# Hybrid decoder layer: the gated linear attention heads' matmuls on the whole 128 x 128 array, two chunks together

## The chip, the core and the metric

The kernel runs on one core of one Trainium2 chip. The engines of the core are named as the profile names them: PE (TensorE, with PEld for its weight loads), DVE (VectorE), ACT (ScalarE), POOL (GpSimd) and SP, which issues DMAs. The metric is the device time of one execution in microseconds (us); lower is better. TensorE's clock is granted at one of two levels, 2.4 GHz (1.00 in the profile) and 1.2 GHz (0.50).

## What is computed

One decoder layer: an input projection, two groups of heads side by side (a gated linear recurrence, HGRN2, and a sparse attention), an output projection, a mixture of experts, and a gate. The change touches the recurrence alone. It has 4 heads of 128 keys and 128 values, and 512 tokens in 8 chunks of 64:

```python
G = jnp.cumsum(chunks(log_f, HG_DK), axis=3)
G_ref, G_last = G[:, :, :, C // 2 - 1:C // 2], G[:, :, :, C - 1:C]
causal = jnp.tril(jnp.ones((C, C), dtype=bool))
a = jnp.einsum('bhntk,bhnsk->bhnts', qc * jnp.exp(G - G_ref), kc * jnp.exp(G_ref - G))
o_intra = jnp.einsum('bhnts,bhnsv->bhntv', jnp.where(causal, a, 0.0), vc)
def step(S, xs):                     # over chunks; k_t = kc*exp(G_last-G), q_t = qc*exp(G)
    q_t, k_t, v_t, d_t = xs
    o_t = jnp.einsum('bhtk,bhkv->bhtv', q_t, S)
    S = d_t[..., None] * S + jnp.einsum('bhtk,bhtv->bhkv', k_t, v_t)
    return S, o_t
```

The output of a head is `o_intra` plus the `o_t` of the scan, then an RMS norm and a gate.

## The kernel before

The layer runs in stages. A first stage projects the 512 tokens onto the columns of the input weights. Each projection is done in three matmuls of reduced-precision parts (`mm3`, lines 181 to 183: high by high, low by high, high by low), 128 x 128 weights against 512 columns; they write tiles named `mm`. The weights come by DMA into `wraw`, ACT makes the high part (`whi`, line 186) and DVE the low part (`wlo`, line 187).

Into this stage the four heads of the recurrence are placed, in the order head 0, head 1, the projection of keys and values (`kv_cols`), head 2, head 3. A list scheduler lays out one static order per engine when the program is built; each engine works strictly through its own row and waits on semaphores where an operand isn't ready. It puts projection matmuls between those of the heads where it expects a wait.

One head (`hg_head`) does this in plain fp32. DVE and ACT make the decayed keys and queries `k1`, `q1`, `k2`, `q2` (lines 368 to 386). Then, for tokens on partitions, two chunks lie side by side in one 128-row tile, the even chunk in rows 0 to 63 and the odd one in rows 64 to 127 (`po = 64 * (n % 2)`):

- line 391: 8 score matmuls, 64 x 64 each, into PSUM tile `at_ps` (named `hx`); line 393: DVE copies the causal part with `copy_predicated` into `AT`, whose other entries were zeroed once;
- line 396: 4 transposes of `k2` into `kt_ps` (the same single PSUM buffer `hx`); line 398: ACT copies them to `kT`, two buffers;
- line 404: 7 matmuls of the state's increments, 64 rows of `kT` against 64 rows of `hv`, into two PSUM tiles `u_ps` in turn; lines 406 and 408: DVE updates the state `St[n]` from `St[n-1]`;
- lines 414 and 415: 7 matmuls `q2` x `St` and 8 matmuls `AT` x `hv`, each for one chunk, into 64 partitions of `o_ps`;
- line 417 (ACT), 419 (DVE), the POOL lines 175 to 178 and line 423 (DVE): norm and gate of the head.

In the records, an fp32 matmul leaves two matmul rows and two weight loads, a transpose one. A row writes a matmul as out<-moving,weights with the array's rows * columns that it uses: `64*64` is a quarter of the array.

Of the kernel before, what the change touches and what calls it, by code (L numbers as in the profile page):

```python
# [10 lines left out]
F32 = mybir.dt.float32  # L11
# [68 lines left out]
def _shape_constants():  # L80
    f = np.float32
    c = np.zeros((128, C_END), f)
    c[:, C_ID:C_ID + 128] = np.eye(128, dtype=f)
    c[:, C_SCAN:C_SCAN + T] = (np.arange(T) % CH != 0).astype(f)[None, :]
    p = np.arange(128)
    c[:, C_CAUS:C_CAUS + 128] = np.where(p[None, :] <= p[:, None], 0.0, NEG)
    n = np.arange(32)
    for tt in range(NT):
        ok = ((tt * 128 + p)[:, None] >= (16 * n + 31)[None, :]) & (n < NCMP)[None, :]
        c[:, C_CADD + 32 * tt:C_CADD + 32 * (tt + 1)] = np.where(ok, 0.0, NEG)  # L90
        c[:, C_C01 + 32 * tt:C_C01 + 32 * (tt + 1)] = ok
    c[:, C_IOTA:C_IOTA + 128] = p[None, :]
    c[:, C_ST:C_ST + 16] = np.array(STARTS[:16])[None, :]
    c[:, C_ST + 16] = 0.0
    c[:, C_ST + 17:C_ST + 32] = np.diff(np.array(STARTS[:16]))[None, :]
    tri = (p[:, None] % 64 <= np.arange(64)[None, :]).astype(np.uint32)
    tri = np.ascontiguousarray(np.broadcast_to(tri[:, None, :], (128, 4, 64)).reshape(128, 256))
    sl = 2.0 ** -np.arange(1.0, QH + 1)
    t = np.arange(T)
    al = np.zeros((2, QH * T + T + 32), f)  # L100
    al[0, :QH * T] = np.repeat(sl, T)
    al[1, :QH * T] = (-sl[:, None] * t[None, :]).reshape(-1)
    al[0, QH * T:QH * T + T] = t
# [51 lines left out]
def _body(ctx, tc, a, out, dbg=None):  # L155
    nc = tc.nc
    V, S, G, PE = nc.vector, nc.scalar, nc.gpsimd, nc.tensor
    act = S.activation
# [11 lines left out]
    hv, nq = hn[:, 0], hn[:, 1]  # L170
# [18 lines left out]
    def flat(ap):  # L189
        return ap.rearrange("p a b -> p (a b)")  # L190
# [10 lines left out]
    with ExitStack() as e2:  # L201
        e0 = ExitStack()
        wst = e2.enter_context(tc.tile_pool(name="wst", bufs=2, side="right", reuse_waits="tile"))
        proj = e0.enter_context(tc.tile_pool(name="proj", bufs=1, reuse_waits="tile"))
# [151 lines left out]
                act(sg[:, tt], gl, AF.Tanh, scale=0.5)  # L356
                V.scalar_tensor_tensor(sg[:, tt], sg[:, tt], 1.0, gl, op0=ALU.add, op1=ALU.mult)

        tri = proj.tile([128, 256], U32, name="tri")
        nc.sync.dma_start(out=tri, in_=a["tri"])  # L360
        ATs = [proj.tile([128, 4, CH], F32, name=f"AT{i}") for i in range(2)]
        for t_ in ATs:
            G.memset(t_, 0.0)
        qc = -0.5 * 128 ** -0.5

        def hg_head(h):
            Gt = lf[:, h].rearrange("p (n c) -> p n c", c=CH)
            V.tensor_tensor_scan(lf[:, h], cst[:, C_SCAN:C_SCAN + T], lf[:, h], 0.0, op0=ALU.mult, op1=ALU.add)
            d1 = hgp.tile([128, NCH, CH], F32, name="d1")
            V.tensor_tensor(d1, Gt, Gt[:, :, CH // 2 - 1:CH // 2].to_broadcast([128, NCH, CH]), op=ALU.subtract)  # L370
            d2 = hgp.tile([128, NCH, CH], F32, name="d2")
            V.tensor_tensor(d2, Gt[:, :, CH - 1:CH].to_broadcast([128, NCH, CH]), Gt, op=ALU.subtract)
            k1 = hgp.tile([128, T], F32, name="k1")
            act(k1, flat(d1), AF.Exp, scale=-1.0)
            q1 = flat(d1)
            act(q1, q1, AF.Exp)
            k2 = flat(d2)
            act(k2, k2, AF.Exp)
            act(Gt, Gt, AF.Exp)
            dk = hgp.tile([128, NCH], F32, name="dk")  # L380
            V.tensor_copy(dk, Gt[:, :, CH - 1])
            q2 = lf[:, h]
            V.scalar_tensor_tensor(q1, q1, qc, qs[:, h], op0=ALU.mult, op1=ALU.mult)
            V.scalar_tensor_tensor(k1, fg[:, h], 1.0, k1, op0=ALU.subtract, op1=ALU.mult)
            V.scalar_tensor_tensor(k2, fg[:, h], 1.0, k2, op0=ALU.subtract, op1=ALU.mult)
            V.scalar_tensor_tensor(q2, q2, qc, qs[:, h], op0=ALU.mult, op1=ALU.mult)
            at_ps = hps.tile([128, 512], F32, name="hx")
            for n in range(NCH):
                po = 64 * (n % 2)
                cs = slice(n * CH, (n + 1) * CH)  # L390
                PE.matmul(at_ps[po:po + 64, (n // 2) * CH:(n // 2 + 1) * CH], lhsT=k1[:, cs], rhs=q1[:, cs], start=True, stop=True)
            AT = ATs[h % 2]
            V.copy_predicated(flat(AT), tri, at_ps[:, :256])
            kt_ps = hps.tile([128, 512], F32, name="hx")
            for tt in range(NT):
                PE.transpose(kt_ps[:, tt * 128:(tt + 1) * 128], k2[:, tt * 128:(tt + 1) * 128], ident)
            kT = hgp.tile([128, NT, 128], F32, name="kT")
            act(flat(kT), kt_ps, AF.Copy)
            St = hgp.tile([128, NCH - 1, 128], F32, name="St")
            u_ps = [hps.tile([128, 512], F32, name=f"u_ps{k}") for k in range(2)]  # L400
            for n in range(NCH - 1):
                po = 64 * (n % 2)
                us = u_ps[n % 2][:, (n // 2) * 128:(n // 2 + 1) * 128]
                PE.matmul(us, lhsT=kT[po:po + 64, n // 2, :], rhs=hv[po:po + 64, n // 2, h * 128:(h + 1) * 128], start=True, stop=True)
                if n == 0:
                    V.tensor_copy(St[:, 0], us)
                else:
                    V.scalar_tensor_tensor(St[:, n], St[:, n - 1], dk[:, n:n + 1], us, op0=ALU.mult, op1=ALU.add)
            o_ps = hps.tile([128, NT, 128], F32, name="o_ps")
            for n in range(NCH):  # L410
                po = 64 * (n % 2)
                o = o_ps[po:po + 64, n // 2, :]
                if n:
                    PE.matmul(o, lhsT=q2[:, n * CH:(n + 1) * CH], rhs=St[:, n - 1], start=True, stop=False)
                PE.matmul(o, lhsT=AT[po:po + 64, n // 2, :], rhs=hv[po:po + 64, n // 2, h * 128:(h + 1) * 128], start=(n == 0), stop=True)
# [812 lines left out]
```

## Time and profile before

| What | us |
|---|---|
| median of 3 runs (1738.06 to 1745.13) | 1738.25 |
| the profiled execution, its own time | 1738.71 |
| its span, first to last instruction | 1737.0 |
| PE busy in the span | 1682.5 |
| stretch with the four heads | 101.74 to 181.44 |

The profile is one execution. Its rows give a start and a duration for each instruction (a row can merge several of one line); PE's rows overlap, since matmuls are pipelined, so the time that one costs is read from start to start. Idle time in front of an instruction stands in square brackets with what ended it; "issue" means that the profile shows nothing that was waited for.

### The profile page before, as it was taken

How to read it: one execution, taken by the hardware profiler on the slowest of the kernel's cores; microseconds unless marked ns; L12 is line 12 of the kernel's file. 1: busy time of each engine (PE TensorE's matmuls, PEld its weight loads, DVE VectorE, ACT ScalarE, POOL GpSimd, SP SyncE). 2: the span in 40 equal slices, each digit the busy share in tenths (PEclk: the TensorE clock that was granted, in tenths of full speed). 3: DMA queues.
4: the chain of work that ended last, by engine and by line, in shares of the span. 5: the costliest groups of instructions: out<-in, count | busy, mean ns of one | idle time of the engine just before them, and what ended most of it. 6: DMA issues, size and time to landing. Idle time of an engine off the chain costs nothing.

```text
span 1737.0 us, 24222 instructions
## 1 busy us (share of the span) xinstructions
PE 1682.5 (97%) x8959; PEld 1430.6 (82%) x8959; DVE 1253.3 (72%) x2442; ACT 742.4 (43%) x1276; POOL 475.8 (27%) x353
## 2 busy tenths in 40 slices
PE   7999999998999999999999999999999999999998
PEld 6866788877885667877899999999999999999987
DVE  5553555556999998594568877787787788888863
ACT  6432555444213985453343333333333333333342
POOL 0001300012000000100035556455554455455510
PEclk9998999889999999999999999999999999999999
DMA  7311022012212679977669888989898999999841
GB/s 254 102 49 27 28 84 63 13 51 96 73 49 62 185 233 267 317 255 253 211 232 331 319 318 324 341 307 324 326 317 315 332 322 325 348 333 336 315 133 49
DMA packets 147303, 374.30 MB, mean 215 GB/s; under 512 B 11670, under 2 KB 60438, under 8 KB 147182
## 3 DMA queue, kind: packets, MB, share of 16 engines
q1 hardware_dynamic: 108608, 232.90, 39.8%
q0 software_dynamic: 38576, 139.86, 22.7%
q8 instruction: 70, 1.15, 0.3%
q14 instruction: 49, 0.40, 0.1%
HBM read 339.42 MB, written 33.29 MB: 215 GB/s over the span
## 4 chain that ended last, share of the span: by engine, by line
PE 80%; DVE 8%; DMA 6%; ACT 3%; issue 2%; SPq 1%; POOL 0%; DVEq 0%; ACTq 0%; POOLq 0%
PE ac L183 9%; PE ac L182 9%; PE ac L181 9%; PE apsum L181 8%; PE apsum L183 8%; PE apsum L182 8%; PE mm L181 5%; PE mm L182 5%; PE mm L183 5%; PE ob L660 2%; DMA ga<-gd 2%; PE apsum L783 2%; DMA ur<-uT 2%; PE pt L657 1%; PE tp L183 1%
## 5 line engine op out<-in xcount | busy, mean ns | idle before, releaser
L183 PE MATMUL ac<-vh,pl 128*128 128x512 f32 x768 | 300.8, 392 | 2.8 <-DVE pl L187 2.8
L181 PE MATMUL ac<-vh,ph 128*128 128x512 f32 x768 | 298.1, 390 | 2.6 <-ACT ph L186 2.6
L182 PE MATMUL ac<-vl,ph 128*128 128x512 f32 x768 | 300.6, 392 | 0.0
L1032 POOL DMA_INDIRECT row<-u,eid x128 | 214.1, 1673 | 310.9 <-DVE hn L1036 243.2
L181 PE MATMUL apsum<-aTh,uh 128*128 128x384 f32 x864 | 290.8, 337 | 2.2 <-ACT ga L788 2.2
L183 PE MATMUL apsum<-aTh,ul 128*128 128x384 f32 x864 | 289.3, 335 | 1.5 <-DVE ul L187 1.4
L182 PE MATMUL apsum<-aTl,uh 128*128 128x384 f32 x864 | 288.7, 334 | 0.0
L1032 POOL DMA_INDIRECT row<-v,eid x128 | 203.7, 1592 | 186.1 <-DVE hn L1044 161.0
L186 ACT ACTIVATE uh<-ur 128x1024 fp32r<-128x1024 f32 x108 | 114.7, 1062 | 281.6 <-PE apsum L182 262.7
L187 DVE TENSOR_TENSOR ul<-ur,uh 128x1024 fp32r<-128x1024 f32 x108 | 132.1, 1224 | 87.6 <-ACT uh L186 87.3
L183 PEld LDWEIGHTS ac<-vh,pl 128*128 128x128 f32 x768 | 144.0, 188 | 34.5 <-DVE pl L187 4.2
L186 ACT ACTIVATE vh<-vr 128x1024 fp32r<-128x1024 f32 x128 | 135.4, 1058 | 86.5 <-PE ac L183 81.6
L181 PEld LDWEIGHTS ac<-vh,ph 128*128 128x128 f32 x768 | 144.1, 188 | 30.9 <-ACT ph L186 3.2
L1044 DVE SCALAR_TENSOR_TENSOR hn<-row,cw__6982,hn 128x1024 f32<-128x1024 f32 x128 | 158.3, 1280 | 14.9 <-DMA row<-v,eid 14.9
L182 PEld LDWEIGHTS ac<-vl,ph 128*128 128x128 f32 x768 | 144.0, 188 | 28.7 <-DVE vl L187 0.5
L181 PEld LDWEIGHTS apsum<-aTh,uh 128*128 128x128 f32 x864 | 162.2, 188 | 6.3 <-ACT ga L788 2.5
L182 PEld LDWEIGHTS apsum<-aTl,uh 128*128 128x128 f32 x864 | 162.3, 188 | 4.0
L183 PEld LDWEIGHTS apsum<-aTh,ul 128*128 128x128 f32 x864 | 162.2, 188 | 2.4 <-DVE ul L187 2.3
L187 DVE TENSOR_TENSOR vl<-vr,vh 128x1024 fp32r<-128x1024 f32 x128 | 156.1, 1219 | 9.9 <-ACT vh L186 9.8
L1036 DVE SCALAR_TENSOR_TENSOR hn<-row,hn 128x1024 f32<-128x1024 f32 x128 | 156.2, 1221 | 5.6 <-DMA row<-u,eid 4.2
L186 ACT ACTIVATE ph<-ga 128x384 fp32r<-128x384 f32 x118 | 62.0, 525 | 202.3 <-DVE ga L1096 147.7
L783 PE MATMUL apsum<-xf,ur 128*128 128x384 f32 x320 | 112.8, 497 | 7.7 <-DMA ur<-uT 7.7
(384 smaller groups left out, 2934.9 us busy)
## 6 DMA issues: line engine op xcount, KB each, us to landing
vr<-v SPq DMA_DIRECT2D x128, 512.0 KB, 5.5
ur<-uT SPq DMA_DIRECT2D x125, 512.0 KB, 6.6
wt<-wd SPq DMA_DIRECT2D x32, 768.0 KB, 7.4
wraw<-wi SPq DMA_DIRECT2D x24, 512.0 KB, 4.6
wd<-hn SPq DMA_DIRECT2D x5, 1664.0 KB, 8.9
wd<-stage SPq DMA_DIRECT2D x5, 1664.0 KB, 9.1
wr<-wq SPq DMA_DIRECT2D x16, 512.0 KB, 3.6
wor<-wo SPq DMA_DIRECT2D x8, 512.0 KB, 3.6
```

Of the source, the lines that this page charges most:

```text
L181: PE.matmul(o, lhsT=lh, rhs=rh, start=first, stop=False)
L182: PE.matmul(o, lhsT=lh, rhs=rl, start=False, stop=False)
L183: return PE.matmul(o, lhsT=ll, rhs=rh, start=False, stop=last)
L186: act(hi, src, AF.Copy)
L187: return V.tensor_tensor(lo, src, hi.bitcast(F32), op=ALU.subtract)
L657: PE.transpose(pt_ps[:, k * 128:(k + 1) * 128], P[:, k * 128:(k + 1) * 128], ident)
L660: PE.matmul(o_ps[:, h], lhsT=pt[:, k * 128:(k + 1) * 128], rhs=kv[:, k, 256 + i * 64:256 + (i + 1) * 64], start=(k == 0), stop=(k == tt))
L783: PE.matmul(o[:, :TD], lhsT=ur[:, c], rhs=xf[:, c], start=c == 0, stop=c == NC - 1)
L1032: G.indirect_dma_start(out=gt, out_offset=None, in_=table, in_offset=bass.IndirectOffsetOnAxis(ap=eid[:, slot:slot + 1], axis=0))
L1036: V.scalar_tensor_tensor(junk, gt, 1.0, xn0, op0=ALU.mult, op1=ALU.mult, accum_out=dots[:, s_:s_ + 1])
L1044: V.scalar_tensor_tensor(ak, gt, cw_[:, s_:s_ + 1], ak, op0=ALU.mult, op1=ALU.add)
```

## The change

The recurrence of a head is done for two chunks (128 tokens) at a time, so that every matmul has 128 rows and 128 columns of the array.

- Scores: 4 matmuls of 128 x 128 instead of 8 of 64 x 64. The mask `tri` becomes block-diagonal and twice as wide (512 columns), and `copy_predicated` takes 512 columns instead of 256.
- `kT` gets a dimension for the chunk's parity. The transposed keys of the even chunk stand in rows 0 to 63 of one half, those of the odd chunk in rows 64 to 127 of the other, and zeros elsewhere. ACT copies the one, DVE the other. `kT` is now one buffer for all heads, zeroed once by POOL. The 7 increments stay 7 matmuls.
- `q2` gets the same treatment along the token columns: it is written in two halves by DVE into a zeroed buffer (the one that was `xsq`), one for all heads, instead of in place over `lf`.
- Output: per 128 tokens one matmul `AT` x `hv` and two (one for the first tile) with the padded `q2` and the states of both chunks, accumulated in the same 128 partitions: 4 and 7 instead of 8 and 7.

```diff
-    tri = (p[:, None] % 64 <= np.arange(64)[None, :]).astype(np.uint32)
-    tri = np.ascontiguousarray(np.broadcast_to(tri[:, None, :], (128, 4, 64)).reshape(128, 256))
+    tri = ((p[:, None] // CH == p[None, :] // CH) & (p[:, None] <= p[None, :])).astype(np.uint32)
+    tri = np.ascontiguousarray(np.broadcast_to(tri[:, None, :], (128, NT, 128)).reshape(128, T))
...
-        ATs = [proj.tile([128, 4, CH], F32, name=f"AT{i}") for i in range(2)]
-        for t_ in ATs:
+        ATs = [proj.tile([128, NT, 128], F32, name=f"AT{i}") for i in range(2)]
+        kT = proj.tile([128, NT, 2, 128], F32, name="kT")
+        q2 = sm.tile([128, D], F32, name="xsq", bufs=1).rearrange("p (t c i) -> p t c i", t=NT, c=2)
+        for t_ in ATs + [kT, q2]:
             G.memset(t_, 0.0)
...
-            q2 = lf[:, h]
-            V.scalar_tensor_tensor(q2, q2, qc, qs[:, h], op0=ALU.mult, op1=ALU.mult)
+            quad = lambda x: x.rearrange("p (t c i) -> p t c i", t=NT, c=2)
+            for c in range(2):
+                V.scalar_tensor_tensor(q2[:, :, c, c * CH:(c + 1) * CH], quad(lf[:, h])[:, :, c], qc, quad(qs[:, h])[:, :, c], op0=ALU.mult, op1=ALU.mult)
             at_ps = hps.tile([128, 512], F32, name="hx")
-            for n in range(NCH):
-                po = 64 * (n % 2)
-                cs = slice(n * CH, (n + 1) * CH)
-                PE.matmul(at_ps[po:po + 64, (n // 2) * CH:(n // 2 + 1) * CH], lhsT=k1[:, cs], rhs=q1[:, cs], start=True, stop=True)
+            for tt in range(NT):
+                ts = slice(tt * 128, (tt + 1) * 128)
+                PE.matmul(at_ps[:, ts], lhsT=k1[:, ts], rhs=q1[:, ts], start=True, stop=True)
             AT = ATs[h % 2]
-            V.copy_predicated(flat(AT), tri, at_ps[:, :256])
+            V.copy_predicated(flat(AT), tri, at_ps)
...
-            kT = hgp.tile([128, NT, 128], F32, name="kT")
-            act(flat(kT), kt_ps, AF.Copy)
+            k3 = kt_ps.rearrange("p (t d) -> p t d", d=128)
+            act(kT[0:64, :, 0], k3[0:64], AF.Copy)
+            V.tensor_copy(kT[64:128, :, 1], k3[64:128])
...
-                PE.matmul(us, lhsT=kT[po:po + 64, n // 2, :], rhs=hv[po:po + 64, n // 2, h * 128:(h + 1) * 128], start=True, stop=True)
+                PE.matmul(us, lhsT=kT[:, n // 2, n % 2], rhs=hv[:, n // 2, h * 128:(h + 1) * 128], start=True, stop=True)
...
-            for n in range(NCH):
-                po = 64 * (n % 2)
-                o = o_ps[po:po + 64, n // 2, :]
-                if n:
-                    PE.matmul(o, lhsT=q2[:, n * CH:(n + 1) * CH], rhs=St[:, n - 1], start=True, stop=False)
-                PE.matmul(o, lhsT=AT[po:po + 64, n // 2, :], rhs=hv[po:po + 64, n // 2, h * 128:(h + 1) * 128], start=(n == 0), stop=True)
+            for tt in range(NT):
+                PE.matmul(o_ps[:, tt], lhsT=AT[:, tt], rhs=hv[:, tt, h * 128:(h + 1) * 128], start=True, stop=False)
+                for c in range(2):
+                    if tt + c:
+                        PE.matmul(o_ps[:, tt], lhsT=q2[:, tt, c], rhs=St[:, 2 * tt + c - 1], start=False, stop=(c == 1))
```

In the changed file the same steps have these lines: scores 393, mask 395, transposes 398, copies of `kT` 400 (ACT) and 401 (DVE), increments 406, states 408 and 410, `AT` x `hv` 413, `q2` x `St` 416, halves of `q2` 389, norm and gate 418, 420 and 424. The scheduler lays the rows out anew. Over all four heads there are 126 projection matmuls from the first score matmul to the end of the stretch before, and the same 126 stand there with the change; they stand in 22 groups behind work of the heads before, in 19 with the change.

On PE, this stood in the middle of head 2's scan before (names as above; `hn` is `hv`, `lf` is `q2`):

```order
L404 MATMUL u_ps_1100<-hn,kT 128x128
L414 MATMUL o_ps<-St,lf 64x128
L404 MATMUL u_ps_1099<-hn,kT 128x128
L415 MATMUL o_ps<-hn,AT_599 64x128
L404 MATMUL u_ps_1100<-hn,kT 128x128
L414 MATMUL o_ps<-St,lf 64x128
L415 MATMUL o_ps<-hn,AT_599 64x128
L414 MATMUL o_ps<-St,lf 64x128
```

And this is the same place on PE with the change (`xsq` is the padded `q2`):

```order
L406 MATMUL u_ps_1087<-hn,kT 128x128
L416 MATMUL o_ps<-St,xsq 128x128
L406 MATMUL u_ps_1086<-hn,kT 128x128
L416 MATMUL o_ps<-St,xsq 128x128
L406 MATMUL u_ps_1087<-hn,kT 128x128
L413 MATMUL o_ps<-hn,AT_599 128x128
L406 MATMUL u_ps_1086<-hn,kT 128x128
L416 MATMUL o_ps<-St,xsq 128x128 x2
```

The sequence is of the same kind, without projection matmuls in it, but all outputs have 128 partitions and `AT` comes half as often.

On DVE, this stood between the scans of head 0 and head 1 before:

```order
L408 SCALAR_TENSOR_TENSOR St<-St,dk,u_ps_785 128x128
L384 SCALAR_TENSOR_TENSOR k_1147<-fg,k_1147 128x512
L406 COPY St<-u_ps_862 128x128
L381 COPY dk<-lf 128x8
L383 SCALAR_TENSOR_TENSOR d_1143<-d_1143,qs 128x512
L419 TENSOR_REDUCE rs<-sq 128x4
L408 SCALAR_TENSOR_TENSOR St<-St,dk,u_ps_863 128x128
L386 SCALAR_TENSOR_TENSOR lf<-lf,qs 128x512
L423 SCALAR_TENSOR_TENSOR hn<-o_ps,rs,sg 128x128 x4
```

And this with the change:

```order
L410 SCALAR_TENSOR_TENSOR St<-St,dk,u_ps_786 128x128
L389 SCALAR_TENSOR_TENSOR xsq<-lf,qs 128x4x64
L401 COPY kT<-hx 64x4x128
L389 SCALAR_TENSOR_TENSOR xsq<-lf,qs 128x4x64
L420 TENSOR_REDUCE rs<-sq 128x4
L408 COPY St<-u_ps_856 128x128
L383 COPY dk<-lf 128x8
L374 TENSOR_TENSOR d_1128<-lf 128x512
L424 SCALAR_TENSOR_TENSOR hn<-o_ps,rs,sg 128x128 x4
L410 SCALAR_TENSOR_TENSOR St<-St,dk,u_ps_857 128x128
```

Head 1's halves of `q2` and its copy of `kT` now stand between the last state of head 0 and the first of head 1, and the gate of head 0 (line 424) ahead of head 1's second state.

## Rows read from the trace of the kernel before

**Rows 1.** The page: busy time, share of the span and rows of each engine.

```profile
PE 1682.5 (97%) x8959; PEld 1430.6 (82%) x8959; DVE 1253.3 (72%) x2442; ACT 742.4 (43%) x1276; POOL 475.8 (27%) x353
```

**Rows 2.** Windows of the heads' stretch: length, busy us (rows) per engine, clock, DMA.

```profile
101.74:130.90 29.16, 29.16 (x164) 17.51 (x163) 16.82 (x40) 9.11 (x16) 1.79 (x3) 1.00 0.22 67
130.90:144.97 14.07, 14.07 (x62) 11.37 (x62) 6.07 (x15) 6.59 (x12) 5.09 (x9) 1.00 0.01 2
144.97:176.33 31.36, 29.88 (x145) 17.25 (x144) 10.32 (x28) 3.44 (x7) 2.76 (x5) 0.75 0.14 37
176.33:181.44 5.11, 5.11 (x14) 4.00 (x13) 2.08 (x7) 1.86 (x3) 3.08 (x6) 0.52 0.07 17
```

**Rows 3.** The same stretch, instructions with tile `mm` alone: PE, PEld, DVE, ACT.

```profile
101.74:181.44 79.70, 37.23 (x126) 24.50 (x125) 0.00 (x0) 4.13 (x6) 0.87 0.14 41
```

**Rows 4.** Timeline of PE in head 0: start us, duration us, line, operation, shapes.

```profile
108.42 0.49 PE L404 MATMUL u_ps<-hn,kT 64*128 64x128 f32 x2
108.84 0.43 PE L414 MATMUL o_ps<-St,lf 128*64 128x128 f32 x2
109.20 0.43 PE L415 MATMUL o_ps<-hn,AT 64*64 64x128 f32 x2
109.56 0.48 PE L404 MATMUL u_ps<-hn,kT 64*128 64x128 f32 x2
```

**Rows 5.** Timeline of PE where projections follow and precede the heads' matmuls.

```profile
114.22 0.50 PE L181 MATMUL mm<-whi,aTh 128*128 128x512 f32 x1
114.56 0.40 PE L182 MATMUL mm<-wlo,aTh 128*128 128x512 f32 x1
114.79 0.39 PE L183 MATMUL mm<-whi,aTl 128*128 128x512 f32 x1
115.11 0.43 PE L414 MATMUL o_ps<-St,lf 128*64 128x128 f32 x2
```

**Rows 6.** Timeline of PE: the 8 score matmuls of head 0 and what follows.

```profile
101.74 0.69 PE L391 MATMUL hx<-d,k 128*64 128x64 f32 x16
102.36 0.50 PE L181 MATMUL mm<-whi,aTh 128*128 128x512 f32 x1
```

**Rows 7.** Timeline of PE in head 3, at the lower clock.

```profile
175.10 0.69 PE L414 MATMUL o_ps<-St,lf 128*64 128x128 f32 x2
175.72 0.69 PE L415 MATMUL o_ps<-hn,AT 64*64 64x128 f32 x2
```

**Rows 8.** Timeline of PE elsewhere: 8 fp32 matmuls on the whole array, and the next row.

```profile
394.27 2.05 PE L516 MATMUL mm<-dg,h 128*128 128x128 f32 x16 [0.87 <-DVE h L501]
396.16 0.60 PE L492 MATMUL mm<-cst,hn 128*128 128x128 f32 x4
```

**Rows 9.** Timeline of PE elsewhere: 4 transposes and the next row.

```profile
204.51 0.60 PE L460 MATMUL kb<-cst,hn 128*128 128x128 f32 x4
204.86 0.37 PE L183 MATMUL mm<-whi,aTl 128*128 128x280 f32 x1
```

**Rows 10.** Groups by line in the stretch: busy us, mean ns | idle before, releasers.

```profile
L408 DVE SCALAR_TENSOR_TENSOR St<-St,dk,u_ps 128x128 f32<-128x128 f32 x24 | 8.3, 345 | 15.3 <-PE u_ps L404 14.9
...
L393 DVE COPY_PREDICATED AT<-tri,hx 128x256 f32<-128x256 uint32 x4 | 1.8, 440 | 4.6 <-PE hx L391 4.6
...
L386 DVE SCALAR_TENSOR_TENSOR lf<-lf,qs 128x512 f32<-128x512 f32 x2 | 1.4, 688 | 0.0
```

**Rows 11.** Timeline of DVE: the gate of head 0, and the work ahead of head 2's states.

```profile
121.58 1.12 DVE L423 SCALAR_TENSOR_TENSOR hn<-o_ps,rs,sg 128x128 f32<-128x128 f32 x4 [1.23 <-POOL rs L178]
...
150.05 0.43 DVE L336 TENSOR_TENSOR kv<-kv,kss 128x256 f32<-128x256 f32 x1 [1.18 <-POOL kss L176]
```

**Rows 12.** Window of the attention stage, columns as in rows 2.

```profile
216.00:300.00 84.00, 81.66 (x589) 68.32 (x588) 45.25 (x89) 49.82 (x113) 3.50 (x5) 1.00 0.24 76
```

**Rows 13.** Timeline of POOL and DVE in the first 40 us.

```profile
0.73 0.56 POOL L363 MEMSET AT<- 128x256 f32 x2 [0.29 <-POOLq L1221]
...
33.13 0.51 DVE L280 TENSOR_SCALAR dg<-cst,r 128x128 f32<-128x128 f32 x2 [2.40 <-PE hx L281]
```

More of the change, by code (lines that the diff above doesn't have):

```diff
@@ L357, in g_cols @@
                 V.scalar_tensor_tensor(sg[:, tt], sg[:, tt], 1.0, gl, op0=ALU.add, op1=ALU.mult)
-        tri = proj.tile([128, 256], U32, name="tri")
+        tri = proj.tile([128, T], U32, name="tri")
         nc.sync.dma_start(out=tri, in_=a["tri"])
-        ATs = [proj.tile([128, 4, CH], F32, name=f"AT{i}") for i in range(2)]
-        for t_ in ATs:
+        ATs = [proj.tile([128, NT, 128], F32, name=f"AT{i}") for i in range(2)]
+        kT = proj.tile([128, NT, 2, 128], F32, name="kT")
+        q2 = sm.tile([128, D], F32, name="xsq", bufs=1).rearrange("p (t c i) -> p t c i", t=NT, c=2)
+        for t_ in ATs + [kT, q2]:
             G.memset(t_, 0.0)
@@ L409, in hg_head @@
             o_ps = hps.tile([128, NT, 128], F32, name="o_ps")
-            for n in range(NCH):
-                po = 64 * (n % 2)
-                o = o_ps[po:po + 64, n // 2, :]
-                if n:
-                    PE.matmul(o, lhsT=q2[:, n * CH:(n + 1) * CH], rhs=St[:, n - 1], start=True, stop=False)
-                PE.matmul(o, lhsT=AT[po:po + 64, n // 2, :], rhs=hv[po:po + 64, n // 2, h * 128:(h + 1) * 128], start=(n == 0), stop=True)
+            for tt in range(NT):
[3 more added lines that the diff above has]
+                        PE.matmul(o_ps[:, tt], lhsT=q2[:, tt, c], rhs=St[:, 2 * tt + c - 1], start=False, stop=(c == 1))
             sq = hgp.tile([128, 512], F32, name="sq")
```

## The prediction, made before the changed kernel was timed

> **What bounds the kernel now.** I read the page first: PE is busy for 1682.5 of 1737.0 us [rows 1], so a microsecond taken from PE where it is the limit should come off the time. Then the windows of the stretch with the four heads, 101.74 to 181.44, 79.7 us in all [rows 2]. PE is busy there in every window but the third, where it waits 1.5 us in all, while DVE has work for 17 of 29 us in the first and 10 of 31 in the third. So the stretch is PE's. The reader should also see the clock column: 1.00 in the first two windows, 0.75 and 0.52 in the last two. Half of the third window and nearly all of the fourth ran at 1.2 GHz, some 20.6 us, although PE was never idle for long: what it did there was the heads' small matmuls.
>
> The timeline of PE gives the price of these [rows 4]. From start to start, a matmul of line 404 takes 0.42 us, one of line 414 or 415 0.36 us. Each uses a half or a quarter of the array, and each neighbour uses another part of it. At the lower clock the same step takes 0.62 us [rows 7]. A projection matmul, four times as wide, takes 0.23 us; but 0.34 us where it follows the heads' work, and the heads' work starts 0.32 us after it [rows 5]. So a change of shape costs 0.11 + 0.09 us around a group of projections.
>
> As a check I build the 79.7 us from these prices: 28 increments of line 404, of which 4 pairs overlap, 24 x 0.42 = 10.1; line 414, 28 x 0.36 = 10.1; line 415, 32 x 0.36 = 11.5; the scores, 4 heads x 0.62 [rows 6] = 2.5; 16 transposes x 0.09 [rows 9] = 1.4; 126 projections [rows 3] x 0.23 = 29.0; 22 groups of them x 0.20 = 4.4; PE's waits 1.5. That is 70.5 us at the full clock. The other 9.2 us are the clock: 20.6 us at half speed would lose up to 10.3.
>
> **The change, part by part.** *Matmuls.* A head has 4 + 7 + 4 + 7 = 22 fp32 matmuls on the whole array in place of 30 on parts of it. Their price is in the trace at another place: 8 of them, of this very shape, take 1.89 us at the full clock, 0.236 us each [rows 8]. All follow each other there with one shape. I take this price; it could be as low as 0.22 (the first of the 8 seems to start late) or as high as 0.36, if it is not the shape that makes the steps of line 414 slow. So 88 x 0.236 = 20.8 us, against 10.1 + 10.1 + 11.5 + 2.5 = 34.2 before. Of these, the scores alone lose: 4 x 4 x 0.236 = 3.8 against 2.5, since their 8 small matmuls overlap [rows 6]. The transposes stay at 1.4, the projections at 29.0.
>
> *Changes of shape.* 19 groups of projections follow the heads' work now. Behind fp32 work I keep the 0.11 us, 2.1 in all; ahead of it I take nothing, as there is no change of shape, with 19 x 0.09 = 1.7 as the other end.
>
> *Waits on DVE.* Here PE gets faster than what feeds it. DVE gets more work: the masked copy has twice the columns, 0.44 to at most 0.88 us [rows 10]; the copy of the odd keys is new, some 0.5 us (between the 0.44 and 0.69 of the same rows); two halves of `q2` cost a little over the 0.69 of one. About 1.2 us per head. In the first window this makes 19 us of DVE work, and PE's sum there (35 projections, 44 matmuls, 8 transposes, 11 groups) is now 20.4 instead of 29.2. An increment must wait until DVE has read the one but one before it (two PSUM tiles), and between two states DVE has another 0.69 us operation in heads 0 and 1. Also, the gate of head 0 waits 1.2 us for POOL and takes 1.1 [rows 11], with head 1's second state queued behind it on DVE; and ahead of head 2's first state stands an operation that waits 1.2 us for POOL [rows 11], now with the odd keys' copy behind it. PE's projections cover much of this. Nothing waited at all would be 0; every one of 12 such steps short by 0.4 us and 2 us at head 2 would be 7. I take 3, twice the 1.5 of before.
>
> *The clock.* I take it as 1.00. The nearest row is the attention stage: for 84 us PE ran short fp32 matmuls over the whole array mixed with wide ones, with small idle times, at 1.00 [rows 12]. What stood in front of both falls here were the parts of head 2 and head 3 with no projections between the quarter-array steps; those are now shorter and denser. It is the weakest step.
>
> *The single buffers.* `kT` and `q2` of a head wait for the last matmuls of the head before. In heads 1 and 3 that puts the copies behind the previous head's output, where 9 and more projections stand on PE; counted in the 3 us.
>
> *At nothing:* two more fills on POOL and wider ones, 128 x 3072 words against the 0.56 us for 512 columns [rows 13], so some 3.4 us. One of them stands between two operations on which the first norm waits, and delays it by 1.1 us; DVE idles 2.4 us behind it for PE's sake [rows 13], which hides that. The mask's DMA doubles by 128 KB in the first 30 us; if its cover is gone, half a microsecond.
>
> *Sum.* 29.0 + 20.8 + 1.4 + 2.1 + 3.0 = 56.3 us in place of 79.7: 23.4 us less. What follows waits for PE's results and moves up as a whole. The profiled execution took 1738.71, so 1715.3; it is 0.5 above the median of the runs, so the median should come out at **1715**.
>
> **A rule that speaks against it.** The score matmuls go at 0.62 / 8 = 0.08 us each, faster than any whole-array fp32 matmul [rows 6 and 8]; the steps of lines 404 to 415 do not [rows 4]. The Trainium skill, "TensorEngine Tiling (Array Packing)", section Overview, says that the array can be split into independent tiles, with up to twofold speed where one dimension is at most 64. By it an estimated 0.12 us (half of a whole-array matmul) would stand for each of the 88 part-tile steps, 10.4 us, and the change would add time. For the scores the trace agrees with it, for the 88 steps it shows 0.36 and more; rival 5 is what it would do here.
>
> **The rivals.**
> 1. *The clock falls again.* For it: the mix is still without wide matmuls in two places of some 4 us, and PE now waits a little ahead of head 2. One fall as long as each of the two before costs half of 9.2, giving 1720; two give 1724.
> 2. *DVE becomes the limit.* For it: 19 us of work against PE's 20.4 in the first window, and the queue order above. Waits of 12 us instead of 3 give 1724. Against it: the third window, where DVE had 10 us of work in 31.
> 3. *It is not the shape.* If a whole-array matmul takes 0.36 us in this place too, because of its operands or its sums in one bank, the 88 cost 31.7 and the time is 1726; with the clock of before as well, 1735, no change. Against it: rows 8.
> 4. *Slower: the scan becomes serial.* If in each of the 28 steps PE waits through 0.42 (increment) + 0.69 (an operation queued on DVE) + 0.35 (state) and only then runs its 0.36 of output, and the gates with their POOL waits, 3 us each, add 9, that is 51.0 + 9, and 29.0 + 3.8 + 1.4 + 2.1 with nothing of it beside: 96.3, so 1755. It turns into a loss from 1.23 us per step on ((79.7 - 9 - 36.3) / 28). Against it: heads 2 and 3 have no such operations between states, and projections do stand beside heads 0 and 1.
> 5. *Packing is lost.* If the 88 part-tile steps overlapped as the scores do, at 0.08 us [rows 6], they would be 7.0 us, and the 72 whole-array matmuls in their place 17.0; with 1.3 more for the scores and 1.5 for waits, 1738.7 + 12.8 = 1751. Against it: rows 4 measure these steps at 0.36 and 0.42.
>
> **How the numbers follow.** About half a per cent (8.7 us) is what a measurement of this kernel can tell from no change: 1729.6 to 1746.9. Forecast 0.63; rival 1 0.18; rival 2 0.10; rival 3 0.06, half of it with the lower clock; rival 4 0.02; rival 5 0.01. The forecast's own range: no waits at all gives 1712, a price of 0.22 takes another 1.4, and other stretches at 1.2 GHz in the layer may shift, as the runs of before differ by 7 us: 1708 at the lower end. At the upper end rivals 1 and 2 reach 1724, and with 3 us more of waits 1727. Outside lie half of rival 3, rivals 4 and 5, and a tenth for errors of the sizes. Faster by over 0.5%: 0.63 + 0.18 + 0.10 + 0.03, less 0.03 for rival 2 at its worst: 0.91. Within: 0.06. Slower: 0.03.
>
> **What would show it.** Right: the steps of lines 406, 413 and 416 are 0.22 to 0.24 us from start to start, the stretch from the first score matmul to the same projection is near 56 us, its clock is 1.00, PE's waits there are about 3 us and come from DVE. Rival 1 shows as a clock below 1.00 in the windows of heads 2 and 3; rival 2 as PE idle before line 406, released by line 401, 408 or 410; rival 3 as steps of 0.36. I would be wrong altogether if the stretch shrinks and the time doesn't: then something after 181 us did not wait for PE.

## The result, and the profile of the changed kernel

| | median us | range, runs |
|---|---|---|
| kernel before | 1738.72 | 1738.06 to 1745.13, 4 |
| changed kernel | 1717.93 | 1714.01 to 1723.99, 4 |

The ratio is 0.9872, with a 95% interval of 0.9852 to 0.9892. The forecast was 1715, 23.4 us less; the medians are 20.8 us apart. The profiled execution of the changed kernel took 1723.99 (span 1722.2), the longest of its four.

The page's busy row, beside [rows 1]:

```profile
PE 1663.2 (97%) x8895; PEld 1430.0 (83%) x8895; DVE 1258.0 (73%) x2450; ACT 742.1 (43%) x1276; POOL 476.8 (28%) x355
```

The windows of the heads' stretch, with the columns of [rows 2]: head 0 and head 1, the projections between, head 2 and head 3, and then the whole, which ends at the same projection as the 79.70 us of before:

```profile
102.56:122.90 20.34, 19.56 (x133) 16.84 (x131) 17.93 (x42) 8.93 (x16) 1.94 (x3) 1.00 0.23 71
122.90:136.80 13.90, 13.90 (x63) 11.51 (x63) 6.69 (x16) 6.57 (x12) 5.09 (x9) 1.00 0.11 36
136.80:156.40 19.60, 16.31 (x117) 14.08 (x116) 13.51 (x33) 3.44 (x8) 2.76 (x5) 1.00 0.23 64
...
102.56:158.33 55.77, 51.70 (x317) 44.05 (x316) 38.81 (x91) 20.23 (x37) 9.98 (x18) 1.00 0.19 57
```

55.77 us stand where 79.70 stood, 23.9 less, and the clock column reads 1.00 where before it read 0.75 and 0.52. PE is idle for 55.77 - 51.70 = 4.07 us. The timeline of PE in head 1's scan gives the new step, beside [rows 4]:

```profile
118.67 0.39 PE L406 MATMUL u_ps<-hn,kT 128*128 128x128 f32 x2
118.89 0.39 PE L416 MATMUL o_ps<-St,xsq 128*128 128x128 f32 x2
119.12 0.39 PE L413 MATMUL o_ps<-hn,AT 128*128 128x128 f32 x2
119.34 0.39 PE L416 MATMUL o_ps<-St,xsq 128*128 128x128 f32 x2
```

0.22 to 0.23 us from start to start, whichever lines follow each other, where before it was 0.42 and 0.36. What PE waited for in the stretch (us in total, times, longest):

```profile
PE u_ps L406 <- DVE kT L401: 1.7, 1, 1.7
PE o_ps L413 <- DVE hn L424: 1.7, 2, 0.9
PE hx L398 <- DVE AT L395: 0.6, 1, 0.6
```

### The profile page after: what moved, and what is told of

Same layout as the page of the kernel before. It is cut to its first block, busy times and chain, and to the rows that moved or that the text cites. A ratio compares the mean times of both kernels' runs of the same rounds, so it can differ in the third digit from the quotient of the medians.

```text
span 1722.2 us, 24101 instructions
## 1 busy us (share of the span) xinstructions
PE 1663.2 (97%) x8895; PEld 1430.0 (83%) x8895; DVE 1258.0 (73%) x2450; ACT 742.1 (43%) x1276; POOL 476.8 (28%) x355
## 4 chain that ended last, share of the span: by engine, by line
PE 51%; issue 16%; DMA 13%; DVE 9%; POOL 8%; ACT 3%; SPq 0%; POOLq 0%; DVEq 0%; ACTq 0%
POOL row L1033 7%; DMA row<-v,eid 6%; PE ac L183 5%; PE ac L181 5%; PE ac L182 5%; PE mm L181 4%; PE mm L182 4%; PE mm L183 4%; PE apsum L181 4%; PE apsum L183 4%; PE apsum L182 4%; DMA ur<-uT 3%; PE ob L661 2%; DMA ga<-gd 1%; PE apsum L784 1%
```

## Experiments

Most kernels here are the changed kernel with one thing altered; all_three alters three, after_again none, and part_rows starts from the kernel before. They are compared by one length that is hardly touched by what happens elsewhere: from the first score row to the first row of `kb<-cst,kv` (line 450 before, 451 with the change, up to 456 in the others), where the work behind the heads begins. "Idle" is that length less PE's busy time, the clock is its mean there; all three come from a window of the profiled execution. A fall of the clock in it costs about the length times (1 - clock).

| Kernel | length us | idle us | clock | time, median us | ratio (95%) |
|---|---|---|---|---|---|
| before | 95.14 | 1.5 | 0.89 | 1738.72 | |
| changed | 71.21 | 4.1 | 1.00 | 1717.93 | 0.9872 (0.9852 to 0.9892) |
| after_again | 71.34 | 4.2 | 1.00 | 1722.66 | 0.9880 (0.9858 to 0.9902) |
| incr_part | 81.42 | 2.9 | 0.96 | 1726.10 | 0.9914 (0.9884 to 0.9943) |
| out_part | 86.58 | 3.8 | 1.00 | 1732.56 | 0.9957 (0.9938 to 0.9975) |
| twice | 88.83 | 4.3 | 0.98 | 1733.90 | 0.9967 (0.9945 to 0.9989) |
| scores_part | 71.03 | 3.8 | 1.00 | 1715.60 | 0.9875 (0.9843 to 0.9908) |
| kt_act | 70.82 | 3.3 | 1.00 | 1715.93 | 0.9857 (0.9837 to 0.9877) |
| late_fill | 73.08 | 4.3 | 0.98 | 1719.69 | 0.9872 (0.9855 to 0.9888) |
| incr_turn | 72.35 | 4.5 | 0.98 | 1721.12 | 0.9871 (0.9852 to 0.9891) |
| all_three | 71.67 | 3.9 | 0.98 | 1716.99 | 0.9879 (0.9857 to 0.9901) |
| part_rows | 75.64 | 3.4 | 1.00 | 1721.87 | 0.9886 (0.9860 to 0.9913) |

Each ratio is against the runs of the kernel before on the same chip, whose medians were 1738.7 to 1741.7; so times are compared through the ratios. Two kernels with added rows ran once: prices in 1774.98, clock_rows in 1911.97 us.

**What a step costs: prices.** Rows of 16 matmuls of 128 columns, put where PE has nothing else to do:

```diff
+ rows = lambda k, po: PE.matmul((b0, b1)[po // 64][:, 0:128], lhsT=W[po:po + 64], rhs=X[po:po + 64], ...)
+ cols = lambda k, po: PE.matmul(b2[po:po + 64, 128:256], lhsT=W[:, 0:64], rhs=X, ...)
+ quart = lambda k, po: PE.matmul(b2[po:po + 64, 256:384], lhsT=W[po:po + 64, 0:64], rhs=X[po:po + 64], ...)
+ full = lambda k, po: PE.matmul((b0, b1)[k % 2][:, 0:128], lhsT=W, rhs=X, ...)
+ mix = lambda k, po: (rows, cols, rows, quart)[k % 4](k, po)
```

> The changed kernel with ten rows of 16 fp32 matmuls of 128 columns added ahead of the last gate's projections, each row headed by one 512-column matmul: whole array; 64 rows, the same half each time; 64 rows, halves in turn; 64 columns, same and in turn; a quarter, same and in turn; the old kernel's sequence (rows, columns, rows, quarter) on the same half and in turn; whole array again. Whole array: 0.22 to 0.24 us a step, 3.6 to 3.8 a row, by every theory. Theory 1 (a step costs more because its neighbour used another shape or place of the array): rows of one shape and one place go at 0.22 or less, the old sequence at 0.36 to 0.42. Theory 2 (a part tile is slow by itself): every part row at 0.36 to 0.42, 5.8 to 6.7 us. Packing (rival 5): the rows with the halves in turn at 0.08 to 0.12, under 2 us, and the old sequence well under 0.36 where the waits of the heads are gone. Time of the whole: 30 to 55 us above the changed kernel.

The timeline of PE there; L1211 is the 512-column matmul at the head of a row:

```profile
1673.28 3.84 PE L1205 MATMUL apsum<-h 64*128 64x128 f32 x32
1677.04 1.13 PE L1211 MATMUL apsum<-h 128*128 128x512 f32 x2
1678.10 2.06 PE L1205 MATMUL apsum<-h 64*128 64x128 f32 x32
1680.08 1.13 PE L1211 MATMUL apsum<-h 128*128 128x512 f32 x2
...
1696.42 0.48 PE L1205 MATMUL apsum<-h 64*128 64x128 f32 x2
1696.84 0.43 PE L1206 MATMUL ac<-h 128*64 128x128 f32 x2
1697.20 0.48 PE L1205 MATMUL apsum<-h 64*128 64x128 f32 x2
1697.62 0.43 PE L1207 MATMUL ac<-h 64*64 64x128 f32 x2
1697.98 0.48 PE L1205 MATMUL apsum<-h 64*128 64x128 f32 x2
...
1700.36 0.79 PE L1205 MATMUL apsum<-h 64*128 64x128 f32 x2
1701.08 0.68 PE L1207 MATMUL ac<-h 64*64 64x128 f32 x2
```

16 matmuls on the same 64 rows take 3.76 us, 0.235 each, no more than the whole ones of [rows 8] (0.236); with the two halves in turn 1.98 us, 0.124 each. The rows of 64 columns and of a quarter read alike: 3.64 the same, 1.90 in turn. Only the last sequence, in the order of the old kernel, takes 0.42, 0.36, 0.42, 0.36: the very steps of [rows 4], with no wait and no other engine at work. So a part tile isn't slow; following another shape is. Theory 2 falls. From about 1700 us on the clock of this sequence reads 0.50 and its steps are 0.72 and 0.62, with PE still busy. The two whole-array rows here took 4.23 and 4.50 us, more than the 3.6 to 3.8 expected, at a mean clock of 0.84 and 0.81, so their price comes from clock_rows below. Packing is real: the Trainium skill, "TensorEngine Tiling (Array Packing)", section Overview, allows up to twice the speed for small matmuls on independent tiles. The trace agrees, 3.76 / 1.98 = 1.9, but only where the shape stays.

**One part undone: incr_part and out_part.**

```diff
- PE.matmul(us, lhsT=kT[:, n // 2, n % 2], rhs=hv[:, n // 2, ...], start=True, stop=True)
+ PE.matmul(us, lhsT=kT[po:po + 64, n // 2, n % 2], rhs=hv[po:po + 64, n // 2, ...], start=True, stop=True)
```

> The changed kernel with the 28 increments alone back on 64 rows of the array, scores and outputs still whole. Theory 1: an increment now stands between two changes of shape, a pair of increment and output costs what it did before, 0.78 in place of 0.45, so the heads get 24 x 0.33 = 8 us longer. Theory 2: only the increments themselves, 28 x (0.42 - 0.22) = 5.6 us, and the outputs beside them stay at 0.22. Packing: 28 x 0.1 = 3 us shorter. The clock: if falls come from part tiles, one of 3 to 10 us may come back at heads 2 or 3; if from stretches without wide matmuls, none, as there is none now.

```profile
148.48 0.39 PE L414 MATMUL o_ps<-hn,AT 128*128 128x128 f32 x2
148.80 0.49 PE L407 MATMUL u_ps<-hn,kT 64*128 64x128 f32 x2
149.21 0.54 PE L417 MATMUL o_ps<-St,xsq 128*128 128x128 f32 x2
```

This is PE in head 2 (output, increment, output). The increment takes 0.41 and the whole-array output in front of it 0.32, though nothing about that output was altered. The length grew by 10.2 us: 3.3 of it is the clock (0.96), and PE is idle for 1.2 less, so 8.1 are left for the steps, as theory 1 has it. The clock fell behind a wait of 1.47 us, and it reads 0.50 from 149.69 to 155.59 us, while PE alternates 64-row increments and whole outputs without a pause. The undone outputs, for both halves `po` in turn:

```diff
- PE.matmul(o_ps[:, tt], lhsT=AT[:, tt], rhs=hv[:, tt, ...], start=True, stop=False)
- PE.matmul(o_ps[:, tt], lhsT=q2[:, tt, c], rhs=St[:, 2 * tt + c - 1], ...)
+ PE.matmul(o, lhsT=q2[:, tt, po // 64, po:po + 64], rhs=St[:, n - 1], start=True, stop=False)
+ PE.matmul(o, lhsT=AT[po:po + 64, tt, po:po + 64], rhs=hv[po:po + 64, tt, ...], start=(n == 0), stop=True)
```

> The changed kernel with the output matmuls alone back as before, 28 of 64 columns and 32 of a quarter, scores and increments still whole. Theory 1: increments at 0.42, outputs at 0.36 again: 60 x 0.36 + 28 x 0.42 = 33.4 in place of 72 x 0.22 = 15.8, 17 us longer. Theory 2: the outputs alone, 60 x 0.36 - 44 x 0.22 = 12 us longer, and the increments stay at 0.22. Packing: 60 x 0.08 = 4.8 in place of 9.7, 5 us shorter. If part tiles make the clock fall, 0.50 comes back in heads 2 and 3, 5 to 9 us more by any theory.

```profile
153.82 0.43 PE L418 MATMUL o_ps<-hn,AT 64*64 64x128 f32 x2
154.18 0.49 PE L406 MATMUL u_ps<-hn,kT 128*128 128x128 f32 x2
154.60 0.43 PE L417 MATMUL o_ps<-St,xsq 128*64 128x128 f32 x2
154.96 0.43 PE L418 MATMUL o_ps<-hn,AT 64*64 64x128 f32 x2
```

The increment is on the whole array and costs 0.42 again, from 154.18 to 154.60. The length is 15.4 us longer, near theory 1's 17; theory 2 had 12 and an increment of 0.22. The clock stayed at 1.00, against what I expected of part tiles.

**The number of steps: twice.** Each increment and each group of outputs is made two times.

```diff
+                for _ in range(2):
-                PE.matmul(us, lhsT=kT[:, n // 2, n % 2], ...)
+                    PE.matmul(us, lhsT=kT[:, n // 2, n % 2], ...)
...
+                for _ in range(2):
-                PE.matmul(o_ps[:, tt], lhsT=AT[:, tt], ...)
+                    PE.matmul(o_ps[:, tt], lhsT=AT[:, tt], ...)
```

> The changed kernel with each increment and each group of output matmuls made twice, 72 whole-array fp32 matmuls more. If PE is the limit at 0.22 us a step and the clock stays: 16 us longer. If waits on DVE are the limit in the scans: under 12, as part of the added work fills the 4 us of waits. If the clock falls because no wide matmul stands between the heads' steps for long, and not because of part tiles: the clock goes to 0.50 in heads 2 and 3, which have twice the length without projections now, and it is 21 to 26 us longer.

The length is 17.6 us longer; less 1.8 for the clock (0.98) and 0.3 for more idle time that is 15.5, against 72 x 0.22 = 16. The waits didn't shrink: they stand where the scans begin, not between the steps.

**What takes the clock: clock_rows.**

```diff
+ mixw = lambda k, po: (full, cols, full, quart)[k % 4](k, po)
+ for fn, alt, m in ((full, 0, 80), (quart, 0, 96), (rows, 64, 192), (mixw, 64, 72), (mix, 64, 56)):
+     for _ in range(16):
+         PE.matmul(b1, lhsT=W, rhs=h1[:, 1, 0:512], start=True, stop=True)
+     for k in range(m):
+         fn(k, alt * (k % 2))
```

> The changed kernel with five long rows of fp32 matmuls of 128 columns added ahead of the last gate's projections, each behind 16 whole-array matmuls of 512 columns: 80 on the whole array; 96 on one quarter, always the same; 192 on 64 rows with the halves in turn; 72 of the sequence whole, 64 columns, whole, quarter (the one of the run out_part); 56 of the old kernel's sequence 64 rows, 64 columns, 64 rows, quarter, with the halves in turn. Each is some 18 to 22 us. What makes the clock fall? Part of the array in use: 0.50 in the quarter's row and in the old sequence, 1.00 in the whole row and, if the halves in turn count as a full array, there. Changes of shape: 0.50 in both sequences, 1.00 in the three rows of one shape. Both together: 0.50 in the old sequence alone, as the run out_part kept 1.00. Steps at the full clock: 0.22, 0.22, 0.11, about 0.33, 0.39.

The windows of the rows: whole, quarter, 64 rows in turn, whole mixed with parts, and, for most of its length, the old kernel's sequence:

```profile
1679.90:1697.70 17.80, 17.80 (x161) 17.80 (x160) 0.00 (x0) 0.00 (x0) 0.00 (x0) 1.00 0.00 1
1711.60:1732.70 21.10, 21.10 (x194) 20.93 (x193) 0.00 (x0) 0.00 (x0) 0.00 (x0) 1.00 0.00 1
1746.60:1768.20 21.60, 21.60 (x385) 21.50 (x384) 0.00 (x0) 0.00 (x0) 0.00 (x0) 1.00 0.01 2
1782.10:1810.00 27.90, 27.90 (x145) 17.38 (x143) 0.00 (x0) 0.00 (x0) 0.00 (x0) 1.00 0.00 1
...
1828.60:1858.00 29.40, 29.40 (x90) 17.19 (x89) 0.00 (x0) 0.00 (x0) 0.00 (x0) 0.50 0.00 1
```

Only the last falls to 0.50, with PE never idle. That it stands last isn't the reason: the same sequence fell in prices too, among rows of 16. Here neither a quarter of the array in one row nor the mixed row of whole tiles, 64 columns and quarters does that; the old scans' mix, all part tiles and a change of shape at each step, does. This agrees with out_part, which had the mixed row's sequence and kept its clock. The 6 us at 0.50 in incr_part, behind a wait, are not explained by it: whole tiles stand between its part tiles. What the chip measures, this doesn't show. The prices are here too, over long rows: 17.80 / 80 = 0.22, 21.10 / 96 = 0.22, 21.60 / 192 = 0.11, 27.90 / 72 = 0.39 (0.33 was expected).

**The old tiles in another order: part_rows.** This is the kernel before; masks, tiles and shapes are its own, and only the order and the opening of the outputs' sums differ.

```diff
+ PE.matmul(flat(o_ps), lhsT=zero, rhs=aTh[:, 0], start=True, stop=False)
+ row(lambda n, po: PE.matmul(us(n), lhsT=kT[po:po + 64, n // 2, :], rhs=vs(n, po), ...), range(NCH - 1))
...
+ row(lambda n, po: PE.matmul(o_ps[po:po + 64, n // 2, :], lhsT=AT[po:po + 64, n // 2, :], rhs=vs(n, po), ...), range(NCH))
+ row(lambda n, po: PE.matmul(o_ps[po:po + 64, n // 2, :], lhsT=q2[:, n * CH:(n + 1) * CH], rhs=St[:, n - 1], ...), range(1, NCH))
+ PE.matmul(flat(o_ps), lhsT=zero, rhs=aTh[:, 0], start=False, stop=True)
```

> The kernel before with every matmul on the part of the array that it had, in another order: a head's 7 increments in one row with the halves in turn, its 8 matmuls of AT and hv in a row, its 7 of q2 and St as far together as the states allow; two whole-array matmuls with zero weights per head open and close the outputs' sums in their bank (8 of 0.23 us that the change doesn't need). If the changes of shape between neighbours are what cost in the kernel before, and not the part tiles: per head 7 x 0.11 + 0.35 for the increments, 8 x 0.11 + 0.35 for AT, 7 x 0.11 + 0.35 (together) to 7 x 0.45 (each alone, between projections) for the states, 0.5 to 0.9 for the zeros, so 4.1 to 6.7 in place of 7.9; with the clock at 1.00 the 79.7 us of the four heads come down to 55 to 66, and the time to 1717 to 1727. If it is the part of the array that is used, by itself, steps and clock stay as before: 76 to 82 us, 1736 to 1744. If PE now waits for the states in heads 2 and 3, 3 us for each is added to the first.

PE in head 1:

```profile
117.21 1.16 PE L412 MATMUL u_ps<-hn,kT 64*128 64x128 f32 x14
118.30 0.50 PE L182 MATMUL mm<-wlo,aTh 128*128 128x512 f32 x1
...
122.43 1.09 PE L418 MATMUL o_ps<-hn,AT 64*64 64x128 f32 x16
123.45 0.66 PE L419 MATMUL o_ps<-St,lf 128*64 128x128 f32 x8
```

7 increments in 1.09 us and 8 of `AT` in 1.02, 0.13 to 0.16 each. The length is 75.64, at a clock of 1.00: 19.5 of the change's 23.9 us, which leaves 60.2 for the four heads, within the 55 to 66 expected. 8 matmuls of zeros, some 0.4 us each, are in it. So most of the gain was to be had without filling the array. The ratio (0.9886) can't be told from the change's.

**The scores: scores_part.** 8 matmuls of 64 x 64 again, into the diagonal blocks, and two masked copies of 64 partitions, both for `po` of 0 and 64.

```diff
- PE.matmul(at_ps[:, ts], lhsT=k1[:, ts], rhs=q1[:, ts], ...)
- V.copy_predicated(flat(AT), tri, at_ps)
+ PE.matmul(at_ps[po:po + 64, cs], lhsT=k1[:, cs], rhs=q1[:, cs], ...)
+ V.copy_predicated(blk(flat(AT)), blk(tri), blk(at_ps))
```

> The changed kernel with the scores alone back as 8 matmuls of 64 x 64 per head, the halves in turn, into the diagonal blocks, and two masked copies of 64 partitions and 256 columns. From the rows of before they cost 0.62 a head against 0.81 now, less the changes of shape of about 0.15 to 0.3 around them: between 0.2 us shorter and 0.1 longer per head, so 0.8 us shorter to 0.4 longer in the stretch. DVE: two copies of 0.44 in place of one of 0.71, 0.7 us more in all, which lengthens PE's wait of 0.6 for AT by 0.2. My term (the scores lose 1.3 us by the change) says 1.3 shorter. In the time, no difference from the changed kernel.

The length is 0.2 us shorter, which is no difference: the scores' row goes from 0.81 to 0.62 us per head, and its neighbours take most of that back.

**The waits on DVE: kt_act, incr_turn.**

```diff
- V.tensor_copy(kT[64:128, :, 1], k3[64:128])
+ act(kT[64:128, :, 1], k3[64:128], AF.Copy)
```

> The changed kernel with the copy of the odd keys on ACT instead of DVE. If DVE's queue is what the increments wait for: PE's wait of 1.74 us ahead of head 2's scan shrinks to under 1 us (DVE must still copy the first state there before a third increment), PE's waits in the stretch go from 4.1 to under 3 us, and the kernel is 1 to 2 us shorter. Rival: ACT's queue takes the same time (two copies of 0.6 us in a row) and the wait only changes its name.

```profile
143.62 0.49 PE L406 MATMUL u_ps<-hn,kT 128*128 128x128 f32 x2 [0.84 <-DVE St L408]
```

The wait ahead of head 2's states is 0.84 instead of 1.74, now for the first state. Idle time fell by 0.7 to 3.3 us, where under 3 was expected, and the length by 0.4: right in kind, but less than the 1 to 2 us expected. Its ratio is the lowest of all, but the intervals overlap.

In incr_turn the 7 increments come first, in a loop of their own that keeps their order:

```diff
+ with tc.issue_after(prev.ins) if n else ExitStack():
+     prev = PE.matmul(us, lhsT=kT[po:po + 64, n // 2, n % 2], rhs=hv[po:po + 64, n // 2, ...], ...)
+ for n in range(NCH - 1):
```

> The changed kernel with the 7 increments of a head on 64 rows of the array again, but one after the other with the halves in turn, ahead of the head's states, instead of each between two outputs. From the added rows of the run on prices: halves in turn cost 0.11 us each inside a row, and a row costs about 0.3 to 0.35 us for its two changes of shape. So a head's increments cost 7 x 0.11 + 0.35 = 1.1 us in place of 7 x 0.22 = 1.6, 1.8 us less over four heads, if all seven stand together; with a group split in two there is no gain. The clock stays at 1.00. Rival: the outputs now come later, behind DVE's row of states, and PE waits for them in heads 2 and 3, by 1 to 3 us per head: no change or slower by up to 4 us.

The length is 1.1 us longer; the clock (0.98) costs 1.4, so at the full clock it would be 0.3 us shorter at most. The 7 increments of head 1 took 1.08 us, as expected, but PE's wait for the gate of head 0 grew from 0.78 to 1.46 us: the outputs come later, as the rival has it, and most of the 1.8 us goes there.

**The start: late_fill.**

```diff
- G.memset(q2, 0.0)
+ G.tensor_scalar(q2, fg[:, 0:2].rearrange("p h (t c i) -> p (h t) c i", c=2, i=128), 0.0, None, op0=ALU.mult)
```

> The changed kernel with one fill on POOL replaced: xsq is zeroed by a product of fg and 0, which can't start before fg is there, and so stands behind the first norm on POOL, not inside it. If that fill delays the start: DVE's first dg moves from 28.20 back to about 27.1, the first PE matmul behind it is 0.9 us earlier, the fall of the clock at 36.4 us goes or moves, and the kernel is 0.9 to 2.6 us shorter. Rival (my step at nothing): DVE waited for PE there, nothing is gained, and the 0.9 us come from something else.

POOL at the start of the changed kernel (profiled execution of the first comparison):

```profile
25.97 0.20 POOL L175 TENSOR_SCALAR r<-ssq 128x4 f32<-128x4 f32 x1 [23.35 <-ACT xsq L273]
26.22 0.96 POOL L365 MEMSET xsq<- 128x1024 f32 x1
27.14 1.02 POOL L176 TENSOR_TENSOR r<-r,mhalf 128x4 f32<-128x4 f32 x1
```

The fill stands inside the norm and delays it by 0.9 us. PE's matmul behind it (line 281) waited 0.16 us for DVE there, as before the change, but in after_again:

```profile
32.84 0.71 PE L281 MATMUL hx<-dg,ones 128*128 128x128 f32 x4 [1.02 <-DVE dg L280]
```

In late_fill DVE's first `dg` is at 26.75 and PE's wait 0.16. So the cover of 2.4 us of idle DVE holds in some executions and falls short by up to 0.9 us in others; the ratio doesn't show it. The fall of the clock at 36 us, which was expected to go or move, is still there (0.50 from 36 to 38 us). The length of late_fill holds another fall, at head 2, which costs 1.5.

**Three edits together: all_three** (those of kt_act, late_fill and incr_turn).

> The changed kernel with the three edits together: odd keys copied by ACT, xsq zeroed late, the increments on 64 rows in turn in one group per head. The stretch: 24 us shorter than before by the change, 0.5 to 1 more by the copy, 0.6 to 1.8 by the group, so 25 to 27; the start 0 to 1 us earlier. The time 1 to 4 us below the changed kernel's, if the outputs don't wait longer for the states, which now come in one row on DVE; if they do (1.5 us for the gate of head 0 in the run incr_turn, in place of 0.8), no difference.

The length is 71.67, with 1.4 lost to a fall of the clock in head 1, behind a wait of 1.9 us for the gate. This is the case of no difference that the expectation names: it is not faster than the change.

**The changed kernel again: after_again.**

> The changed kernel itself, for its spread. The stretch with the heads is the same program and should again be 24 us shorter than before; the profiled execution of the first time gave some 8 us back behind it, in three places: about 3.6 us at 653 to 680, 1.7 at 1565, 1.6 at 1671. If these belong to the changed kernel, they are here again and the median stays at 1718. If they are an accident of one execution, some are absent here, the profiled execution is at 1714 or below, and the median of more runs lies at 1714 to 1718.

The length is the same within 0.13 us. The median, 1722.66, is above the 1714 to 1718 expected, but that of the kernel before is higher in this comparison too (1741.74); the ratios, 0.9872 and 0.9880, agree. One part of the difference between executions is the attention stage behind the heads, the same program in both of these (windows of the first profile of the changed kernel, then of kt_act):

```profile
290.00:372.00 82.00, 75.91 (x429) 63.94 (x427) 43.16 (x99) 39.01 (x126) 9.80 (x15) 0.83 0.13 39
```

```profile
290.00:372.00 82.00, 73.40 (x468) 60.61 (x468) 48.76 (x111) 44.44 (x140) 10.73 (x18) 0.98 0.16 46
```

A clock of 0.83 in one and 0.98 in the other; the profile of before reads 0.86 in that window. From the first row of `kb` to the first of line 517 (`mm<-dg,h`) the one takes 198.3 us, the other 190.9. So the same instructions behind the heads can take 7.4 us less in one execution than in another. The second part is the stage whose weights come by DMA. Between the same two rows of PE, before and after_again:

```profile
676.17:888.57 212.40, 203.35 (x1144) 174.59 (x1142) 135.57 (x237) 93.29 (x118) 11.49 (x12) 1.00 0.78 251
```

```profile
654.70:869.55 214.85, 205.07 (x1143) 175.74 (x1142) 136.31 (x237) 93.41 (x118) 11.52 (x12) 0.99 0.78 250
```

It is 2.4 us longer here, 5.0 in the first profile of the changed kernel, and 1.8 to 6.6 in the profiles of all the other kernels, against the one of before. The third part is the rest of the kernel: from the second of these rows to the last instruction it takes 848.4 us before and in kt_act, but 851.6 and 851.5 in the two profiles of the changed kernel, with a wait of 1.3 and 1.1 us for `ph` near 1565 us and a fall of the clock near 1671 us in both. So the three losses that the expectation names came again, the first of them smaller.

## Why the prediction came out as it did

**The step** (88 x 0.236 = 20.8): right, at 0.224 or 19.7, 1.1 us less. I took it from a row of another stage, [rows 8]; what counted was that the shape stays the same, as twice, prices and the undone parts show. Rival 3 is out.

**The clock** (1.00, the weakest step): right in the profiled execution. I named the quarter-array steps without projections between them as what stood in front of the falls; a row of quarter tiles alone keeps 1.00, and it is the old sequence, with its changes of shape, that falls (clock_rows and prices). More length without projections, in twice, brought one short fall. Rival 1 isn't quite out: behind a wait of 1.5 to 1.9 us for DVE a fall comes in some executions and not in others. The same window of head 2's scan in the first profile of the changed kernel and in prices, where the scan starts 0.8 us earlier:

```profile
143.50:147.30 3.80, 3.76 (x32) 3.73 (x33) 2.37 (x7) 0.00 (x0) 0.00 (x0) 1.00 0.28 75
```

```profile
143.50:147.30 3.80, 3.80 (x22) 3.80 (x21) 1.65 (x6) 0.00 (x0) 0.00 (x0) 0.55 0.18 63
```

**The waits** (3 us): 4.07 us, and mostly where I put them. The 1.74 is at head 2, where the copy of the odd keys stands on DVE behind an operation that waits for POOL; the others are `o_ps`, held by the gate of the head before (0.78 and 0.92), and `AT` (0.63). Rival 2's 12 us didn't come, and neither did rival 4's serial scan: once a head's scan runs, PE doesn't wait between its steps.

**Changes of shape** (2.1 us): what remains of 55.77 is 55.77 - 29.0 - 19.7 - 1.4 - 4.1 = 1.6. **Scores** (a loss of 1.3): 4 x (0.81 - 0.62) = 0.8, and 0.2 with what stands around them.

**DVE's added work** (1.2 us per head): over the compared length it went from 39.49 to 44.31 us, 1.2 per head. **At nothing** (the fill): true in the first profile, up to 0.9 us in others.

**Sum**: 56.3 forecast, 55.77 found. That it came so near is in part luck: the steps were 1.1 us too dear and the waits 1.1 us too cheap. By the rule on the clock above, 95.14 x 0.11 = 10.5 of the 23.9 us are the clock (9.2 in the prediction's check), PE idles 2.6 more, and so some 16.0 are the steps and their changes of shape.

**Packing** (rival 5): I said that the trace shows 0.36 and more for the 88 steps. It shows that for their old order only; part_rows gets 0.13 to 0.16 from the same tiles. Rival 5's condition wasn't met. Its 0.08 came from the score matmuls, with 64 moving columns; with 128 the rows of prices take 0.12 and those of clock_rows 0.11.

**The step that failed** is the last: "what follows waits for PE's results and moves up as a whole". The medians moved by 20.8 and 19.1 us (1741.74 to 1722.66 in the second comparison), 2.6 to 4.3 less than the sum. The profiled executions lost more: their spans are 14.8 us (first profile) and 16.0 (after_again) shorter than the 1737.0 of before, where the compared length alone gave 23.9 and 23.8. Ahead of it, the heads begin 0.8 and 2.3 us later (102.56 and 104.08 in place of 101.74), with a fall of the clock at 36 us that the profile of before doesn't have. Just behind it, a fall of the clock at 179.7 us costs 1.3 (from the wait for `hn` to the first row of `sc` 12.68 us in place of 11.36); it came in most profiles of changed kernels, behind a wait of 1.93 us that stands in the profile of before too, without a fall. The DMA-fed stage gives back 5.0 and 2.4, the rest of the kernel 3.2 and 3.0. The last of these came alike in both profiles and not in kt_act. All of it rests on a single profile of before, so how much belongs to the change, and how much to the execution, stays open; in the medians it is about the size of the spread.

## To carry to other kernels

Before padding small matmuls to the whole array, look at the order in which they stand: matmuls of one part-tile shape with the halves in turn took 0.11 us each, whole ones 0.22, and where the shape changed at every step each took 0.36 to 0.42, whole or part. Where dependences force shapes to alternate, make them one shape, even with zeros; where they can stand in rows, part tiles cost PE no more per step, though no run here was clearly faster with them than the change. Price such a step from a row of that very shape elsewhere in the trace, and allow for a few microseconds of such a gain not showing in the time: here that was 2.6 to 4.3 of 23.4.

## What the runs showed of the hardware

- A whole-array fp32 matmul between two part tiles costs 0.42 us, as much as the part tile that it replaced (out_part). A 64-row matmul makes the whole-array one in front of it dearer too, 0.32 for 0.22 (incr_part).
- The clock fell to 0.50 while PE was never idle, in the sequence of 64 rows, 64 columns, 64 rows and a quarter (clock_rows, and prices too), and not in a row of quarter tiles of 21.1 us.
- With the halves in turn, 64-row matmuls go at twice the rate of the same tiles in one place: 16 in 1.98 us against 3.76 (prices), and 192 in 21.6 us (clock_rows).
